# Splitting the merge's weights during the second token group instead of at their first use

## Chip, core and metric

The kernel runs on 1 core of one Trainium2 chip. The metric is device time in microseconds (us) of one execution. The time before is the median of three runs.

## What is computed

One layer of an encoder trunk on 2048 prompt tokens and 8 x 16 decode tokens (17 tiles of 128 tokens), all in float32. Every token gets one wide projection; three branches (a gated convolution, a gated linear recurrence, a causal stick-breaking attention) turn it into `o_a`, `o_b`, `o_c`; the merge at the end combines them. The change concerns the weights of the merge, `w_branch` (1536 x 1024) and `w_out` (1024 x 1024):

```python
    h = rms_norm(x, norm_g[l])
    (a_x, ..., s_z, m_a, m_b, m_c) = split_cols(h @ w_in[l])
    ...
    wb = w_branch[l]
    y_a = o_a @ wb[:W_CONV]
    y_b = o_b @ wb[W_CONV:W_CONV + W_HG]
    y_c = o_c @ wb[W_CONV + W_HG:]
    m = jax.nn.sigmoid(m_a) * y_a + jax.nn.sigmoid(m_b) * y_b + jax.nn.sigmoid(m_c) * y_c
    return x + m @ w_out[l], conv_new, S_new.astype(x.dtype), k, v
```

## The kernel before

**Products of float32 numbers.** Each float32 matrix is kept as two parts of type fp32r: `hi`, the value rounded by a cast on ScalarE (ACT), and `lo`, the rest, subtracted on VectorE (DVE). The helper `split` does both (lines 175 and 176). A product is then three passes on TensorE (PE): hi x hi, hi x lo, lo x hi.

**Weights.** `wload` fetches a weight piece of 512 KB. At its first use it comes as float32 into a staging buffer `wst` (two of them) and is split into a buffer `w` that holds both parts (1024 KB, three of them). `wkeep` then stores `w` to a tensor `W` in device memory, and later uses of the same piece load the two parts from there, without a split. Every fourth load of a kept piece goes into the two staging buffers instead of a `w` (the counter `turns`).

**Stages.** Three token groups (`GROUPS`: 5, 6 and 6 tiles) run the projection one after another, each in 64 jobs (72 weight pieces) on two chunks of tokens, so 128 turns to a group. The weights of the projection are split in the first group. The merge follows: four groups of tokens (`PGROUPS`: 5, 4, 4 and 4 tiles), each with 12 branch jobs (`bjob`, matmuls on line 1391, gating on DVE on lines 1397 to 1400) and 4 output jobs (`ojob`, matmuls on line 1422, one DVE addition on line 1430). Each merge group uses the same 20 weight pieces (12 of `w_branch`, 8 of `w_out`). Before the change the first merge group splits them, and the other three load parts.

**Work beside the jobs.** Generators run a slice of other work at each `yield` of a job: `hbg` the recurrence, `bg` the attention. During the second token group `bg` is the decode tokens' attention; from the third on it is the prompt's attention, in four query blocks, which the merge needs one by one. A step of it, for one tile of queries against up to 512 keys, is: two matmuls into `z` (lines 329, 330), two sigmoids on ACT (333, 335), a scan along the keys and a product on DVE (342, 347), four transposes on PE into `tp` (310), a copy on ACT (311), and later matmuls into `pv` (359). Each link waits for the one before.

**What sets the order.** The code only gives priorities. When the program is built, a scheduler lays out every engine's instructions in one fixed order, from the order of the code and its own reckoning of when data and buffers are ready. On the chip each engine, and the DMA queue of SyncE (SP), which issues all transfers, goes through its list strictly in that order and waits where something is missing. So a change to one stage's loads can also change which instructions stand next to each other.

Of the kernel before, what the change touches and what calls it, by code (L numbers as in the profile page):

```python
# [8 lines left out]
F32 = mybir.dt.float32  # L9
F32R = mybir.dt.float32r  # L10
# [6 lines left out]
P = 128  # L17
# [81 lines left out]
def trunk(ctx: ExitStack, tc: tile.TileContext, x_prompt, x_sample, cache_conv, state_hgrn, cache_k, cache_v,  # L99
# [3 lines left out]
    nc = tc.nc  # L103
# [25 lines left out]
    dram = ctx.enter_context(tc.tile_pool(name="dram", bufs=1, space=DRAM))  # L129
# [43 lines left out]
    def split(hi, lo, src, eng=None):  # L173

        first = nc.scalar.copy(hi, src)  # L175
        return first, (eng or nc.vector).tensor_tensor(lo, src, hi.bitcast(F32), ALU.subtract)  # L176
# [8 lines left out]
    kept = {}  # L185
    turns = [0]

    def wload(pieces, key):


        out = []
        for n, v in enumerate(pieces):
            a, b = v.shape[1], v.shape[2]
            if (key, n) in kept:
                turns[0] += 1
                if turns[0] % 4 == 0:

                    hl = []
                    for i in range(2):
                        x = wp.tile([P, a, b], F32, tag="wst", name="wst", bufs=2)  # L200
                        nc.sync.dma_start(x, kept[key, n][:, i].rearrange("p (a b) -> p a b", a=a).bitcast(F32))
                        hl.append(x.bitcast(F32R))
                    out.append((*hl, None))
                    continue
            w = wp.tile([P, 2, 1024], F32R, tag="w", name="w")
            hi, lo = (w[:, i].rearrange("p (a b) -> p a b", a=a) for i in range(2))
            if (key, n) in kept:
                nc.sync.dma_start(w.bitcast(F32), kept[key, n].bitcast(F32))
            else:
                st = wp.tile([P, a, b], F32, tag="wst", name="wst", bufs=2)  # L210
                nc.sync.dma_start(st, v)
                with ExitStack() as order:
                    if len(kept) < 1 and n:

                        for x in prep.last:
                            order.enter_context(tc.issue_after(x.ins))
                    split(hi, lo, st)
            out.append((hi, lo, w))
        return out
# [3 lines left out]
    def wkeep(out, key):  # L223
        for n, (_, _, w) in enumerate(out):
            if (key, n) not in kept:
                kept[key, n] = dram.tile([P, 2, 1024], F32R, name=f"W{len(kept)}")
                nc.sync.dma_start(kept[key, n].bitcast(F32), w.bitcast(F32))
# [519 lines left out]
    def build_vectors():  # L747
        nc.sync.dma_start(qg_bc, q_norm_g[0].partition_broadcast(P))
        nc.sync.dma_start(kg_bc, k_norm_g[0].partition_broadcast(P))

        vrow = g0p.tile([17, P], F32, tag="mtmp", name="vrow", bufs=2)
        nc.sync.dma_start(vrow[0:12], conv_w[0].rearrange("j (b p) -> (j b) p", p=P))
        nc.sync.dma_start(vrow[12:16], hg_lb_logits[0].rearrange("(h p) -> h p", p=P))
        nc.sync.dma_start(vrow[16:17], hg_norm_g)
        pvec = ps_tp()
        nc.tensor.transpose(pvec[:, 0:17], vrow, idf[0:17, 0:17])
        nc.vector.tensor_copy(vec, pvec[:, 0:17])
# [10 lines left out]
    def build_bound():  # L768
        lmax = const.tile([P, 4], F32, name="lmax")
        nc.vector.tensor_copy(lmax, vec[:, 12:16])  # L770
        lexp = const.tile([P, 4], F32, name="lexp")
        nc.vector.tensor_tensor(lexp, vec[:, 12:16], lmax, ALU.subtract)
        ebase = const.tile([P, 1], F32, name="ebase")
        nc.vector.memset(ebase, 2.718281828459045)
        nc.gpsimd.tensor_tensor(lexp, ebase.broadcast_to([P, 4]), lexp, ALU.pow)
        lsum = const.tile([P, 4], F32, name="lsum")
        nc.vector.reciprocal(lsum, lexp)
        lsm = const.tile([P, 4], F32, name="lsm")
        nc.vector.tensor_tensor(lsm, lexp, lsum, ALU.mult)
        nc.vector.tensor_tensor(lb, lsm, lsm, ALU.subtract)  # L780
        nc.vector.tensor_scalar(omlb, lb, -1.0, 1.0, ALU.mult, ALU.add)
# [22 lines left out]
    def build_rev():  # L804
        nc.gpsimd.memset(rev, 0.0)
        nc.gpsimd.affine_select(rev, rev, pattern=[[1, P]], base=1 - P, channel_multiplier=1,
                                compare_op=ALU.not_equal, fill=1.0)
# [39 lines left out]
    def build_hist():  # L847
        nc.gpsimd.memset(uhist, 0.0)
        nc.gpsimd.memset(shist, 0.0)
        nc.gpsimd.memset(cstage, 0.0)  # L850
        nc.sync.dma_start(cstage[0:16], cache_conv[0].rearrange("b t c -> (b t) c"))
# [407 lines left out]
    def run_late(cost):  # L1259
        for x in late:  # L1260
            x[0] -= cost
        for x in list(late):
            if x[0] <= 0:
                try:
                    x[0] = next(x[1])
                except StopIteration:
                    late.remove(x)

    def run_jobs(g, jobs):
        nonlocal prep  # L1270
        nxt = None
        n = len(jobs)
        ws = {}

        def weights(i):
            if i < n and i not in ws:
                ws[i] = wload(*jobs[i][0])

        order = [(i, ci) for i in range(2, n - 2) for ci in range(2)]
        begin = [(0, 0), (1, 0), (0, 1), (1, 1)] if g else [(0, 0), (0, 1), (1, 0), (1, 1)]  # L1280
        order = (begin + order
                 + [(n - 2, 0), (n - 1, 0), (n - 2, 1), (n - 1, 1)])
        for at_, (i, ci) in enumerate(order):
            weights(i)
            if g or at_:
                weights(i + 1)
            if not g and at_ == 0:
                prep.advance()
            if not g and at_ == 2:

                with tc.issue_after(rstd_at[0].ins), tc.issue_after(prep.last[1].ins):
                    build_vectors()
                    build_hist()
                    build_rev()
                    build_bound()
                    build_masks()
                    build_selectors()
            hT = prep.chunk(ci) if g or at_ > 1 else lambda ti, ci=ci: prep.tile(ci, ti)
            left = len(order) - at_
            if left == 5 and g + 1 < len(GROUPS):  # L1300
                nxt = Prepare(g + 1)
            for cost in jobs[i][1](ws[i], ci, hT):
                if at_ < 2:
                    prep.advance()
                    prep.advance()
                if nxt and (left <= 2 or nxt.ready < 0 and len(nxt.xt) < 3 or left <= 3 and not nxt.scaled):
                    nxt.advance()
                run_late(cost)
                hbg.run(cost * RATE_H)
                bg.run(cost * RATES[g] * jobs[i][2])  # L1310
            if ci == 0 and g < len(GROUPS) - 1:
                wkeep(ws[i], jobs[i][0][1])
        while late:
            run_late(1e9)
        hbg.drain()
        prep = nxt

    for g in range(len(GROUPS)):
        run_jobs(g, group_jobs(g))
        if g == 0:  # L1320
            p0.close()
            bg.add(sample_attention())
        if g == 1:
            prep.chunk(0)
            bg.drain()
            p01.close()
            open_attention()
            for qi in range(4):
                bg.add(attention(qi), key=qi)
# [4 lines left out]


    p3 = ctx.enter_context(tc.tile_pool(name="p3", bufs=1))
    wb = w_branch[0]
    wo = w_out[0]
    GMAX = max(sum(len(c) for c in pg) for pg in PGROUPS) * P

    def branch_w(x, dp):
        return ([wb[x * 512:(x + 1) * 512, dp * 256:(dp + 1) * 256].rearrange("(k p) m -> p k m", p=P)],
                ("branch", x, dp))

    def out_w(s):
        v = wo[:, s * 256:(s + 1) * 256].rearrange("(k p) m -> p k m", p=P)
        return [v[:, 0:4], v[:, 4:8]], ("out", s)

    def merge_jobs(gi):
        pg = PGROUPS[gi]  # L1350
# [85 lines left out]
    alljobs = []  # L1436
# [10 lines left out]
    ws = {0: wload(*alljobs[0][0])}  # L1447
    for i, (_, compute) in enumerate(alljobs):
        if i + 1 < len(alljobs):
            ws[i + 1] = wload(*alljobs[i + 1][0])  # L1450
        wkeep(ws[i], alljobs[i][0][1])
        for cost in compute(ws.pop(i)):
            bg.run(cost * RATE_M)
    bg.drain()
# [29 lines left out]
```

## Time and profile before

| what | value |
|---|---|
| median of 3 runs | 2918.34 us (2917.2 to 2919.45) |
| the profiled execution | 2918.2 us, of which the span from first to last instruction is 2916.1 us |
| mean granted TensorE clock | 0.997 |
| bytes moved by DMA | 624.58 MB, mean 214 GB/s |
| loads of kept weights | 153 of 1024 KB into `w`, 102 of 512 KB into `wst` (two for one piece) |
| stores of kept weights | 92 of 1024 KB |
| first merge matmul (line 1391) | 2188.8 us |
| last split of a weight starts | 2458.8 us |

The profile gives each engine's busy time. PE is matmuls, PEld their weight loads, which overlap with them; PEclk is the granted clock, 1.00 at full speed. "[1.36 <-DVE sp]" behind an instruction means that its engine stood idle 1.36 us before it, until DVE had written `sp`.

### The profile page before, as it was taken

The page shows a single profiled execution, that of the slowest core. Times are in us where ns is not written, and L with a number is a line of the kernel's source. Part 1 is how long each engine was busy: PE and PEld are TensorE (multiplying, and loading weights), DVE is VectorE, ACT ScalarE, POOL GpSimd, SP SyncE. Part 2 cuts the span into 40 slices and gives each one's busy share as a digit, 9 for nine tenths or more (in the row PEclk, how much of TensorE's full clock was granted, in tenths as well). Part 3 has the DMA queues.
Part 4 walks back from the last instruction along what each step waited for, and adds up shares of the span by engine and source line. Part 5 has one row for each costly group of instructions (what it writes and reads, how often), then busy time and mean ns, then how long its engine had stood idle before and what let it go on. Part 6 is the DMA issues. An engine that isn't in the chain of part 4 may idle for free.

```text
span 2916.1 us, 51581 instructions
## 1 busy us (share of the span) xinstructions
PE 2881.3 (99%) x19511; PEld 2673.5 (92%) x19511; DVE 1542.4 (53%) x3284; ACT 1020.2 (35%) x2371; POOL 322.5 (11%) x787
## 2 busy tenths in 40 slices
PE   9999999999999999999999999999998999999999
PEld 8999999999999999999999999999986777788888
DVE  5454644641352523345444748366575866867743
ACT  4333223242222222114333443334443444444420
POOL 3100000120100000002221111101011011110100
PEclk9999999999999999999999999999999999999999
DMA  8877777777556564536774454434438867888876
GB/s 307 306 259 247 234 229 242 246 237 246 187 185 213 175 220 149 166 138 192 248 219 159 153 160 156 149 128 166 131 118 276 271 227 257 297 264 262 274 258 218
DMA packets 355481, 624.58 MB, mean 214 GB/s; under 512 B 31929, under 2 KB 242706, under 8 KB 323874
## 3 DMA queue, kind: packets, MB, share of 16 engines
q1 hardware_dynamic: 355234, 621.29, 64.9%
q8 instruction: 155, 2.54, 0.3%
q14 instruction: 92, 0.75, 0.1%
HBM read 423.99 MB, written 197.17 MB: 213 GB/s over the span
## 4 chain that ended last, share of the span: by engine, by line
PE 75%; DVE 3%; DMA 1%; issue 1%; ACT 1%; POOL 0%; SPq 0%; DVEq 0%; POOLq 0%; ACTq 0%
PE acc L710 32%; PE acc L721 9%; PE acc L1391 9%; PE acc L1422 6%; PE pv L359 4%; PE tp L310 4%; PE z L329 2%; PE z L330 2%; PE z L1040 1%; DVE pr L342 1%; PE tp L458 1%; PE pv L522 1%; DMA xt<-in_x_prompt_dram 0%; PE z L476 0%; PE hg L1087 0%
## 5 line engine op out<-in xcount | busy, mean ns | idle before, releaser
L710 PE MATMUL acc<-hx,w 128*128 128x384 f32 (+1 forms) x6816 | 1254.7, 333 | 0.0
L710 PEld LDWEIGHTS acc<-hx,w 128*128 128x128 f32 x6816 | 1107.3, 188 | 22.2 <-issue 15.2
L721 PE MATMUL acc<-w,hx 128*128 128x256 f32 x2544 | 329.5, 284 | 1.7 <-DVE gm L1134 0.7
L342 DVE TENSOR_TENSOR_SCAN pr<-snb,carry 128x513 f32<-128x513 f32 x192 | 246.3, 1283 | 154.1 <-ACT snb L333 152.6
L721 PEld LDWEIGHTS acc<-w,hx 128*128 128x128 f32 x2544 | 311.4, 188 | 5.0 <-DVE hx L176 1.6
L311 ACT COPY aT<-tp 128x512 f32<-128x512 f32 (+2 forms) x320 | 167.0, 525 | 339.8 <-PE tp L310 331.6
L1391 PE MATMUL acc<-o,w 128*128 128x512 f32 (+2 forms) x1224 | 256.3, 360 | 5.6 <-DVE gate L1399 3.3
L710 PE MATMUL acc<-hx,wst 128*128 128x384 f32 x1248 | 247.3, 344 | 0.0
L1391 PEld LDWEIGHTS acc<-o,w 128*128 128x128 f32 x1224 | 207.0, 191 | 43.0 <-DVE gate L1399 9.0
L333 ACT ACTIVATE snb<-z 128x512 f32<-128x512 f32 (+2 forms) x320 | 172.5, 539 | 182.9 <-PE z L330 180.0
L710 PEld LDWEIGHTS acc<-hx,wst 128*128 128x128 f32 x1248 | 215.6, 188 | 6.4 <-issue 3.7
L347 DVE TENSOR_TENSOR sp<-sp,pr 128x512 f32<-128x512 f32 (+2 forms) x320 | 194.8, 610 | 25.4 <-PE tp L310 0.5
L342 DVE TENSOR_TENSOR_SCAN pr<-snb,one 128x129 f32<-128x129 f32 (+3 forms) x128 | 114.5, 895 | 133.9 <-POOL snb L338 133.2
L310 PE MATMUL tp<-idf,sp 128*128 128x128 f32 x1088 | 173.2, 275 | 6.3 <-DVE sp L347 5.1
L1422 PE MATMUL acc<-w,mh 128*128 128x256 f32 x896 | 175.4, 285 | 3.2 <-DVE w L176 2.4
L335 ACT ACTIVATE sp<-z 128x512 f32<-128x512 f32 (+2 forms) x320 | 171.8, 537 | 0.0
L176 DVE TENSOR_TENSOR w<-wst,w 128x1024 fp32r<-128x1024 f32 x92 | 112.5, 1224 | 111.7 <-ACT w L175 111.7
L310 PEld LDWEIGHTS tp<-idf,sp 128*128 128x128 f32 x1088 | 132.3, 142 | 30.5 <-ACT aT L311 8.6
L1422 PEld LDWEIGHTS acc<-w,mh 128*128 128x128 f32 x896 | 142.9, 188 | 11.6 <-issue 5.0
L1174 ACT ACTIVATE gm<-acc 128x384 f32<-128x384 f32 (+1 forms) x144 | 68.2, 474 | 232.9 <-PE acc L710 198.1
L359 PE MATMUL pv<-aT,Vt 128*64 128x512 f32 (+3 forms) x640 | 137.3, 541 | 1.6 <-ACT aT L311 1.6
L329 PE MATMUL z<-Kt,Q 128*128 128x512 f32 (+2 forms) x320 | 130.9, 410 | 2.7 <-ACT sp L335 2.6
(300 smaller groups left out, 3474.7 us busy)
## 6 DMA issues: line engine op xcount, KB each, us to landing
w<-W SPq DMA_DIRECT2D x153, 1024.0 KB, 5.3
W<-w SPq DMA_DIRECT2D x92, 1024.0 KB, 5.0
wst<-W SPq DMA_DIRECT2D x102, 512.0 KB, 5.0
wst<-in_w_in_dram SPq DMA_DIRECT2D x72, 512.0 KB, 6.3
GM<-gm SPq DMA_DIRECT2D x120, 192.0 KB, 3.4
Kt<-KT SPq DMA_DIRECT2D x160, 128.0 KB, 3.6
o<-OX SPq DMA_DIRECT2D x72, 256.0 KB, 4.7
gate<-GM SPq DMA_DIRECT2D x72, 256.0 KB, 4.1
```

The source lines that it names most:

```text
L310: nc.tensor.transpose(tp[:, j * P:(j + 1) * P], sp[:, j * P:(j + 1) * P], idf)
L311: nc.scalar.copy(aT[:, e, 0:nb, i * P:(i + 1) * P], tp[:, :w].rearrange("p (b q) -> p b q", q=P))
L329: nc.tensor.matmul(z[:, :w], Q1[:, i * P:(i + 1) * P], Kt[:, :w], start=True, stop=False)
L333: nc.scalar.activation(sn[:, 512 - w:512], z[:, :w], AF.Sigmoid, scale=-0.125)
L335: nc.scalar.activation(sp[:, :w], z[:, :w], AF.Sigmoid, scale=0.125)
L342: nc.vector.tensor_tensor_scan(pr[:, 512 - w:513][:, ::-1], s_in, s_in, one if diag else carry[e][i], ALU.mult, ALU.bypass)
L347: nc.vector.tensor_tensor(sp[:, :w], sp[:, :w], pr[:, 513 - w:513], ALU.mult)
L359: nc.tensor.matmul(pv[64 * e:64 * e + 64, c0:n], Vt[:, j, e], aT[:, e, j, c0:n], start=first and j == 0, stop=last and j == nb - 1, skip_g ...
L710: nc.tensor.matmul(acc[:, :n], w[0][a][:, k], hT[b][:, k, :n], start=k == 0 and i == 0, stop=k == KB - 1 and i == 2)
L721: nc.tensor.matmul(acc[:, :256], hT[b][:, k, ti * P:(ti + 1) * P], w[k // 4][a][:, k % 4], start=k == 0 and i == 0, stop=k == KB - 1 and i ...
L1391: nc.tensor.matmul(acc[:, :n], w[0][a][:, k, dd * P:(dd + 1) * P], box[x][b][:, k, sl], start=k == 0 and i == 0, stop=k == 3 and i == 2)
L1422: nc.tensor.matmul(acc[:, :256], box["l" if b else "h"][:, k, ti * P:(ti + 1) * P], w[k // 4][a][:, k % 4], start=k == 0 and i == 0, stop= ...
```

## The change

The 20 pieces of the merge are loaded as float32, split and stored while the second token group runs. A new generator `split_merge_weights` works on half a piece at a time (512 numbers to a partition), in three turns: load, split, store. It has its own two buffers, one float32 half `mwx` and one pair of parts `mwp`. There are 40 halves, so 120 turns, and `run_jobs` calls it once in each of the turns 4 to 123 of the second group. The pool `mw` is opened after the first group and closed after the second. In the merge every load of a weight, in the first group too, is then one of kept parts, and the loop no longer calls `wkeep`. Lines below the insertion move by 28 to 29: the merge's matmuls stand on lines 1420 and 1451, the new loads on 1292, the new stores on 1297.

```diff
+    def split_merge_weights():
+
+        mw = mwx.enter_context(tc.tile_pool(name="mw", bufs=1, side="right"))
+        yield
+        for pieces, key in [branch_w(x, dp) for x in range(3) for dp in range(4)] + [out_w(s) for s in range(4)]:
+            for n, v in enumerate(pieces):
+                kept[key, n] = dram.tile([P, 2, 1024], F32R, name=f"W{len(kept)}")
+                a, b = v.shape[1], v.shape[2]
+                for half in range(2):
+                    x = mw.tile([P, 512], F32, tag="mwx", name="mwx")
+                    nc.sync.dma_start(x.rearrange("p (a b) -> p a b", b=b), v[:, half * a // 2:(half + 1) * a // 2])
+                    yield
+                    w = mw.tile([P, 2, 512], F32R, tag="mwp", name="mwp")
+                    split(w[:, 0], w[:, 1], x)
+                    yield
+                    nc.sync.dma_start(kept[key, n][:, :, half * 512:(half + 1) * 512].bitcast(F32), w.bitcast(F32))
+                    yield
...
+            if g == 1 and 4 <= at_ < len(order) - 4:
+                next(splitting, None)
...
         if g == 0:
             p0.close()
+            next(splitting)
             bg.add(sample_attention())
         if g == 1:
             prep.chunk(0)
             bg.drain()
+            for _ in splitting:
+                pass
+            mwx.close()
             p01.close()
...
             ws[i + 1] = wload(*alljobs[i + 1][0])
-        wkeep(ws[i], alljobs[i][0][1])
         for cost in compute(ws.pop(i)):
```

(`branch_w` and `out_w` are moved up unchanged.)

**Where instructions stand now.** PE's list is the same up to a few places at the start of the second group, then the same until the merge begins, and differs over the first merge group; the later merge groups stand as before. The first place is on PE in the first merge group, behind about 150 branch matmuls. `z` and `tp` belong to attention steps, `pv` to their last product, `acc` to the merge. Before:

```order
L1391 MATMUL acc<-o,w 128x384 x12
L330 MATMUL z<-Kt,Q_24210 128x512
L329 MATMUL z<-Kt,Q_24209 128x512
L330 MATMUL z<-Kt,Q_24210 128x512
L310 MATMUL tp<-idf,sp 128x128 x4
L359 MATMUL pv<-aT,Vt 64x512
L329 MATMUL z<-Kt,Q_24209 128x512
L330 MATMUL z<-Kt,Q_24210 128x512
L310 MATMUL tp<-idf,sp 128x128 x12
L359 MATMUL pv<-aT,Vt 64x512 x4
L1391 MATMUL acc<-o,w 128x256 x12
```

and now, as many branch matmuls into the merge:

```order
L1420 MATMUL acc<-o,wst 128x256 x6
L310 MATMUL tp<-idf,sp 128x128 x4
L1420 MATMUL acc<-o,w 128x384 x6
L329 MATMUL z<-Kt,Q_25628 128x384
L330 MATMUL z<-Kt,Q_25629 128x384
L1420 MATMUL acc<-o,w 128x384 x6
L310 MATMUL tp<-idf,sp 128x128 x4
L1420 MATMUL acc<-o,w 128x256 x6
L329 MATMUL z<-Kt,Q_25628 128x512
L330 MATMUL z<-Kt,Q_25629 128x512
L1420 MATMUL acc<-o,w 128x256 x6
```

Before, four sets of transposes and the products stood together with no merge matmul between them; now six merge matmuls stand between the links of a step.

The second place is SP's list where the merge begins (`wst<-in_w_branch_dram` are the float32 weights, `W<-w` their store, `o` the branch outputs, `gate` the gates). Before:

```order
L211 DMA wst<-in_w_branch_dram 128x4x256
L1175 DMA GM<-gm 128x384
L211 DMA wst<-in_w_branch_dram 128x4x256
L287 DMA Kt<-KT 64x512
L1361 DMA o<-OX 128x640 x8
L227 DMA W_25099<-w 128x2048
L1383 DMA gate<-GM 128x640 x2
```

and now:

```order
L208 DMA w<-W_7901 128x2048
L1175 DMA GM<-gm 128x384 x2
L287 DMA Kt<-KT 64x512 x2
L1175 DMA GM<-gm 128x384
L1098 DMA out_dram<-Sn 128x128
L291 DMA Vt<-VV 128x4x128
L208 DMA w<-W_8363 128x2048
L1175 DMA GM<-gm 128x384
L182 DMA OX<-oh 128x256
L182 DMA OX<-ob 128x256
L201 DMA wst<-W_8911 128x1024
```

The weights of the first four branch jobs are now issued ahead of the merge, among the last stores of the third token group, and no store of weights follows.

The third place is ACT's list in the second token group (`vf` are evacuations of a projection job, `at` and `od` belong to the decode attention). One piece of the difference:

```order
 L836 COPY vf<-acc 128x256 x2
 L175 CAST kt<-hg 128x256
-L501 COPY at__8105<-tp 128x384
-L836 COPY vf<-acc 128x256 x4
+L501 COPY at__8128<-tp 128x384
+L836 COPY vf<-acc 128x256 x3
+L175 CAST mwp<-mwx 128x512
+L836 COPY vf<-acc 128x256
 L527 COPY od<-pv 128x128
```

A cast of half a weight piece now stands between two evacuations of the accumulators.

More of the change, by code (lines that the diff above doesn't have):

```diff
@@ L1267, in run_late, with branch_w, out_w @@
                     late.remove(x)
+    wb = w_branch[0]
+    wo = w_out[0]
+    mwx = ExitStack()
+    def branch_w(x, dp):
+        return ([wb[x * 512:(x + 1) * 512, dp * 256:(dp + 1) * 256].rearrange("(k p) m -> p k m", p=P)],
+                ("branch", x, dp))
+    def out_w(s):
+        v = wo[:, s * 256:(s + 1) * 256].rearrange("(k p) m -> p k m", p=P)
+        return [v[:, 0:4], v[:, 4:8]], ("out", s)
+    def split_merge_weights():
[14 more added lines that the diff above has]
+                    yield
+    splitting = split_merge_weights()
     def run_jobs(g, jobs):
@@ L1336, in trunk @@
     p3 = ctx.enter_context(tc.tile_pool(name="p3", bufs=1))
-    wb = w_branch[0]
-    wo = w_out[0]
     GMAX = max(sum(len(c) for c in pg) for pg in PGROUPS) * P
[L1341 to L1347, printed above, removed]
     def merge_jobs(gi):
```

## Prediction

> **What bounds the kernel now.** I read the page's first part, then a table of the stages, then, where PE stands idle, the waits and the timeline. The page:
>
> ```profile
> span 2916.1 us, 51581 instructions
> PE 2881.3 (99%) x19511; PEld 2673.5 (92%) x19511; DVE 1542.4 (53%) x3284; ACT 1020.2 (35%) x2371; POOL 322.5 (11%) x787
> ```
>
> PE is busy 2881.3 of 2916.1 us, and the change takes no matmul away, so all there is to win is PE's idle time (34.8 us) and what a lowered clock costs. Where these lie, by stage (stretch in us, its length, then busy time of PE, PEld, DVE, ACT, POOL with counts, the granted clock, DMA share, GB/s):
>
> ```profile
> 620.00:1330.00 710.00, 710.00 (x5298) 690.46 (x5297) 256.60 (x746) 182.37 (x489) 43.10 (x84) 1.00 0.57 186
> 2180.00:2190.00 10.00, 7.81 (x41) 5.03 (x41) 9.23 (x10) 9.08 (x17) 0.55 (x3) 0.99 0.88 279
> 2190.00:2360.00 170.00, 155.00 (x880) 123.06 (x879) 115.32 (x186) 69.65 (x141) 20.88 (x51) 0.96 0.80 263
> 2360.00:2470.00 110.00, 107.93 (x731) 91.91 (x732) 72.44 (x92) 49.22 (x92) 9.88 (x31) 1.00 0.76 254
> 2470.00:2847.00 377.00, 377.00 (x2220) 306.45 (x2219) 256.47 (x342) 151.19 (x302) 34.25 (x111) 1.00 0.81 269
> ```
>
> The first row is the second token group, where the splits go: PE never idle. Rows two to four are the first merge group and its outputs, where the splits come from: idle 2.19, 15.00 and 2.07 us, over half of all idle time, in a tenth of the span. The last row is the rest of the merge with the same attention beside it and no splits: idle 0. Who is waited for, between 2180 and 2470 us (total, times, longest):
>
> ```profile
> PE tp L310 <- DVE sp L347: 5.1, 7, 1.4
> PE acc L1391 <- DVE gate L1399: 3.3, 2, 2.4
> PE z L329 <- ACT sp L335: 2.6, 3, 2.1
> PE acc L1422 <- DVE w L176: 2.4, 2, 1.3
> PE acc L1391 <- DVE mp L1397: 2.2, 2, 1.9
> PE pv L359 <- ACT aT L311: 1.6, 3, 0.7
> ```
>
> Only the fourth row names a split. The others are the links of an attention step and the gating behind them on DVE. The timeline shows the first kind (start, duration, engine, line):
>
> ```profile
> 2223.12 0.69 DVE L347 TENSOR_TENSOR sp<-sp,pr 128x512 f32<-128x512 f32 x1
> 2223.73 1.28 DVE L342 TENSOR_TENSOR_SCAN pr<-snb,carry 128x513 f32<-128x513 f32 x1
> 2223.96 1.08 PE L310 MATMUL tp<-idf,sp 128*128 128x128 f32 x4 [1.36 <-DVE sp L347]
> 2225.12 0.69 DVE L347 TENSOR_TENSOR sp<-sp,pr 128x512 f32<-128x512 f32 x1
> 2225.96 1.09 PE L310 MATMUL tp<-idf,sp 128*128 128x128 f32 x4 [0.91 <-DVE sp L347]
> 2227.72 3.42 PE L359 MATMUL pv<-aT,Vt 128*64 128x512 f32 x8 [0.68 <-ACT aT L311]
> ```
>
> DVE needs 1.28 + 0.69, about 2 us, for a step; PE's transposes of it are done in half of that, and then PE has nothing: its list holds twelve transposes and the products in a row (the order of before above). So PE goes at DVE's pace, and the clock falls too:
>
> ```profile
> 2190.00:2200.00 10.00, 10.00 (x47) 7.19 (x48) 6.24 (x7) 2.97 (x6) 0.00 (x0) 0.84 1.02 356
> 2220.00:2230.00 10.00, 6.72 (x22) 3.00 (x24) 6.29 (x8) 4.39 (x9) 0.00 (x0) 0.70 1.07 277
> 2230.00:2240.00 10.00, 9.77 (x52) 6.25 (x49) 2.42 (x5) 2.87 (x8) 2.27 (x7) 0.96 0.16 64
> 2340.00:2350.00 10.00, 7.58 (x35) 5.58 (x34) 6.23 (x14) 3.61 (x9) 2.47 (x6) 0.84 0.37 116
> ```
>
> The clock is below full by 1.6, 3.0, 0.4 and 1.6 us in these four slices, 6.6 in all. Idle time at a low clock must not be counted twice: 3.28 x 0.30 + 2.42 x 0.16 = 1.4 off, so 5.2 us. What can be regained in 2190 to 2470 is thus 15.0 + 2.1 + 5.2 = 22.3 us.
>
> [...]
>
> **The change part by part.**
>
> *1. The first merge group loses its splits.* Rows of the splits, whole and as an existing 512-wide split has them (busy, mean ns | idle before), and DVE's and ACT's work on `wst` in the stretch:
>
> ```profile
> L175 ACT CAST w<-wst 128x1024 fp32r<-128x1024 f32 x92 | 96.8, 1052 | 66.5 <-PE acc L710 24.4 <-DMA wst<-in_w_in_dram 12.8 <-DMA wst<-in_w_branch_dram 11.7
> L176 DVE TENSOR_TENSOR w<-wst,w 128x1024 fp32r<-128x1024 f32 x92 | 112.5, 1224 | 111.7 <-ACT w L175 111.7
> L175 ACT CAST oth<-ot 128x512 fp32r<-128x512 f32 x16 | 9.9, 620 | 54.0 <-DVE ot L366 54.0
> L176 DVE TENSOR_TENSOR ot<-ot,oth 128x512 fp32r<-128x512 f32 x16 | 11.0, 689 | 7.5 <-ACT oth L175 7.5
> ...
> 2190.00:2360.00 170.00, 0.00 (x0) 0.00 (x0) 13.28 (x11) 12.74 (x12) 0.96 0.80 263
> ```
>
> 20 pieces x 1.224 = 24.5 us leave DVE and 20 x 1.052 = 21.0 us leave ACT, beside PE, so nothing of it counts by itself. ACT also no longer stands in line for the float32 pieces: 11.7 us of idling in its list, with attention steps behind.
>
> *2. PE's list is laid out anew in this group.* This is the part that counts. Of the two lists above, the new one keeps six merge matmuls between the links of a step. I went through all of both lists: from the merge's start on, the old one has eleven places with three or more attention steps, or twelve or more transposes, in a row without a merge matmul; the new one has one, at the very start, where PE waits for `o` in both. Bounds for what comes back: 0 (the waits only move) and all 22.3 us. The nearest row for the new state is 2470 to 2847: the same interleaving, no idle time, clock 1.00, with DVE at 256.47 / 377 = 68%. The first group would have DVE at (115.32 - 13.28) / (170 - 20) = 68%, so it should come near that row. A second reading: PEld is busy 123.06 / 170 = 72% here and 306.45 / 377 = 81% there; at 81% the 170 us would shrink by 18.6.
>
> [...]
>
> I take 80% of 22.3, 17.8 us, and leave 4.5 for what I expect to stay: the 1.6 of clock after the wait for `o`, and places where gates come late, since ninety merge matmuls now stand in a row where `o` has landed:
>
> ```profile
> 2200.69 1.35 DVE L1397 TENSOR_TENSOR mp<-acc,gate 128x384 f32<-128x384 f32 x3 [4.06 <-DMA gate<-GM]
> ...
> w<-W SPq DMA_DIRECT2D x153, 1024.0 KB, 5.3
> W<-w SPq DMA_DIRECT2D x92, 1024.0 KB, 5.0
> gate<-GM SPq DMA_DIRECT2D x24, 320.0 KB, 4.8
> wst<-in_w_branch_dram SPq DMA_DIRECT2D x12, 512.0 KB, 5.8
> kc<-in_cache_k_dram SPq DMA_DIRECT2D x64, 256.0 KB, 4.1
> ```
>
> *3. Transfers of the first merge group.* 20 x 512 KB in and 20 x 1024 KB out become 20 x 1024 KB in: 30 MB become 20, and SP has 20 issues fewer that waited for DVE. A load of parts lands after 5.3 us, a float32 piece after 5.8 and then two splits' time. The first four jobs' loads stand ahead of the merge. Price 0; if a job's weights came late each time, 5.3 us x a few jobs, which is in the high end.
>
> *4. The wait at 2180 to 2190 us.* The first merge matmul needs `o`, loaded once the last gates are stored, in both orders. PE gets two more attention steps into the wait. Bounds: 0 to 2.2 us regained, a loss of as much if a step ends after `o` has come. I take 0.
>
> *5. The second token group gains the splits.* 40 casts x 0.620 = 24.8 us on ACT, 40 x 0.689 = 27.6 us on DVE, 80 transfers (40 x 256 KB in, as the row of 4.1 us, 40 x 512 KB out). ACT goes from 182 to 207 and DVE from 257 to 284 us of 710, 29% and 40%. The cover is PE's own work: ACT's evacuations wait for PE there, not PE for them. SP's weight loads likewise wait for PE to free a buffer, so they are early. In that group:
>
> ```profile
> ACT gm L1174 <- PE acc L710: 102.0, 41, 4.5
> SPq L208 <- PE acc L710: 95.3, 23, 10.7
> ```
>
> ACT is early by 102.0 / 41 = 2.5 us on the mean. A cast of 0.62 us and a wait for its load (in the first group 12.8 us for 72 casts, 0.18 each) fit in. The new store waits on SP for DVE's half, one turn after it was given out; behind it stand weight loads with 4.1 us to spare (95.3 / 23). With no cover at all the price is 40 x (0.62 + 0.18) = 32 us; nothing excludes a microsecond of gain or loss from the few matmuls moved at this group's start. I take +0.5.
>
> *Sum.* -17.8 + 0 + 0.5 = -17.3 us on the profiled execution of 2918.2 us (span 2916.1, 2.1 around it), which stands 0.1 under the median of 2918.34: 2901 us.
>
> **The rivals.**
>
> *A, as summed:* 2901, own range 2893 to 2908.
>
> *B, the denser list meets transfers:* with PE quicker, gates (two buffers, 4.8 us each) or parts become what PE waits for. For it: DMA share 0.80 and the 4.06 us wait. Against it: 2470 to 2847 has a share of 0.81 and no idle time. Half of the 17.8 is lost: 2909.
>
> *C, the waits move:* five of six rows of waits name attention and gating, not splits; if DVE's chain stays in PE's way, only row four (2.4 us) and its clock go: 2915. For it: the rows. Against it: the chain of 2 us a step is the same from 2470 on, where it costs nothing.
>
> *D, slower: ACT blocks in the second group.* A cast waits for `mwx`, whose load can stand on SP behind a weight load that waits for PE, up to 10.7 us; evacuations stand behind the cast on ACT, and PE stops when its two accumulators are full. It decides from 17.8 / 40 = 0.45 us of PE per half; at 1 us each the time is 2901 + 40 = 2941. For it: the single `mwx` and the cast between evacuations. Against it: ACT's 2.5 us, and the first group's 0.18.
>
> **How the numbers follow.** A 0.65, B 0.15, C 0.12, D 0.08. The likeliest is A, 2901. Faster than 0.2% (5.8 us, about what a measurement of this kernel can tell, so below 2912.5): A, and nearly all of B, 0.78. Within 0.2%: nearly all of C and the rest of B, 0.14. Slower: D, 0.08. The range reaches from everything regained with the wait of part 4 and its clock (2918.2 - 22.3 - 2.2 - 2, about 2891) up to B with some loss in the second group (2913); that leaves out C and D, 0.2.
>
> **What would show it.** In the changed kernel's profile: PE's idle time and clock in the first merge group near those of 2470 to 2847; no row of PE waiting for a split after the first token group; PE busy 710 of 710 in the second group, with ACT and DVE 25 and 28 us up; the same times for the stages after the first merge group. B would show as PE or DVE waiting for `gate` or `w` at the merge, C as the same waits for `sp` and `aT`, D as idle time of PE in the second group with ACT's casts waiting for `mwx`.

## The result and the profile after

| | before | after |
|---|---|---|
| median of 4 runs of each on one chip | 2917.77 us | 2902.40 us (2896.27 to 2903.30) |
| ratio | | 0.9943, 95% interval 0.9926 to 0.9961 |
| profiled execution, its span | 2918.2, 2916.1 us | 2896.3, 2894.6 us |

15.4 us faster by the medians, 21.5 by the two spans: the profiled execution of after is the quickest of its four, 6 us under the other three. The total is near the 2901 forecast by luck: the merge gained about twice as much as the sum said, and the second token group gave nearly half of it back. The first lines of the page after:

```profile
span 2894.6 us, 51726 instructions
PE 2864.3 (99%) x19511; PEld 2671.5 (92%) x19511; DVE 1547.5 (53%) x3304; ACT 1025.5 (35%) x2391; POOL 317.0 (11%) x787
```

PE has the same 19511 matmuls and is busy 17 us less. So "busy" held time that was no work, and the page alone can't say where it went. Landmarks do: when a line's instructions start for the last or the first time. Rows of lines and tiles (count, min/median/max ns, first to last start); before, the last transpose of a token group's input (the third's, which is done while the second group ends), the last projection matmul, the first branch matmul, the first output matmul:

```profile
L629 PE MATMUL tp<-idf,xt x136: 270/272/329, 8.0 to 1349.6; 128*128 128x128 f32 x136
L710 PE MATMUL acc<-hx,wst x1248: 331/337/449, 663.4 to 2180.0; 128*128 128x384 f32 x179
L1391 PE MATMUL acc<-o,w x1224: 274/390/667, 2188.8 to 2861.3; 128*128 128x512 f32 x92, 128*128 128x384 f32 x43, 128*128 128x256 f32 x40
L1422 PE MATMUL acc<-w,mh x896: 274/281/390, 2358.1 to 2911.2; 128*128 128x256 f32 x180
```

and after:

```profile
L629 PE MATMUL tp<-idf,xt x136: 270/273/421, 8.0 to 1366.5; 128*128 128x128 f32 x136
L710 PE MATMUL acc<-hx,wst x1248: 331/337/444, 668.0 to 2196.2; 128*128 128x384 f32 x179
L1420 PE MATMUL acc<-o,w x1080: 274/392/482, 2206.2 to 2839.7; 128*128 128x512 f32 x108, 128*128 128x384 f32 x38, 128*128 128x256 f32 x34
L1451 PE MATMUL acc<-w,mh x816: 274/281/387, 2343.1 to 2889.6; 128*128 128x256 f32 x164
```

| stretch | before | after | change |
|---|---|---|---|
| start to the end of the second group (last x-transpose) | 1349.6 | 1366.5 | +16.9 |
| from there to the last projection matmul | 830.4 | 829.7 | -0.7 |
| to the first branch matmul | 8.8 | 10.0 | +1.2 |
| to the first output matmul | 169.3 | 136.9 | -32.4 |
| to the end | 558.0 | 551.5 | -6.5 |

**Where the second group lost 17 us.** Its row in the table of stages, which was 710 of 710 busy, and PE's waits between 560 and 1380 us:

```profile
620.00:1330.00 710.00, 698.20 (x5197) 676.11 (x5196) 270.45 (x754) 198.51 (x517) 43.54 (x84) 1.00 0.68 226
```

```profile
PE hg L827 <- DVE kt L176: 7.1, 4, 3.0
PE tp L1089 <- ACT ktm L1053: 2.5, 3, 1.2
PE tp L629 <- DVE xt L619: 2.5, 3, 1.3
PE tp L629 <- DVE hx L176: 2.1, 1, 2.1
PE acc L721 <- ACT kn L815: 1.3, 1, 1.3
```

PE now waits for small jobs of ACT and DVE that used to be early: 18.1 us with the smaller rows, against 5.6 before. The clock adds 3.4 us at most, an estimate from 2 x 3.41 us at one half (at 591 and 793 us); before, it is at full speed throughout this group. The waits of ACT and DVE name what holds those two:

```profile
ACT mwp L175 <- DMA mwx<-in_w_branch_dram: 56.6, 23, 5.6
ACT mwp L175 <- DMA mwx<-in_w_out_dram: 44.4, 16, 4.7
DVE mwp L176 <- ACT mwp L175: 108.0, 36, 25.0
```

39 of the 40 casts stand at the head of ACT's list before their data has landed: 101.0 us in 39 waits, 2.6 us each. DVE stands behind the same casts; no run separates its list from ACT's. The timeline of one case (start, duration, engine, line):

```profile
634.88 0.62 ACT L175 CAST mwp<-mwx 128x512 fp32r<-128x512 f32 x1 [3.61 <-DMA mwx<-in_w_branch_dram]
635.40 0.38 ACT L813 ACTIVATE sq<-acc 128x256 f32<-128x256 f32 x1
635.93 0.39 ACT L175 CAST kt<-hg 128x256 fp32r<-128x256 f32 x1
637.38 0.41 DVE L817 TENSOR_REDUCE ssq<-sq 128x4 f32<-128x256 f32 x1
637.49 0.53 SPq L1297 DMA_DIRECT2D W<-mwp  x1
638.11 0.56 SPq L1292 DMA_DIRECT2D mwx<-in_w_branch_dram  x1
639.20 0.42 DVE L820 TENSOR_TENSOR kn<-kn,rr 128x256 f32<-128x256 f32 x1 [1.41 <-POOL rr L234]
...
640.00 0.41 DVE L176 TENSOR_TENSOR kt<-hg,kt 128x256 fp32r<-128x256 f32 x1
640.47 0.44 PE L827 MATMUL hg<-idf,kn 128*128 128x128 f32 x2 [2.99 <-DVE kt L176]
642.60 0.62 ACT L175 CAST mwp<-mwx 128x512 fp32r<-128x512 f32 x1 [4.07 <-DMA mwx<-in_w_branch_dram]
```

ACT waits 3.61 us for a half's load, and only behind its cast come the squares `sq` and the cast of `kt`. DVE's sum `ssq`, GpSimd's `rr`, DVE's `kn` and the rest of `kt` follow one by one, and PE stands idle for 2.99 us until `kt` is done. That this wait of PE goes back to ACT's is read from the order of the lists. Meanwhile SP issues the next load right behind the last half's store, and ACT waits 4.07 us for it; behind that wait PE has no idle time until 648 us, so not every wait of ACT costs PE. Nor are the splits spread as the code's turns are:

```profile
L175 ACT CAST mwp<-mwx x40: 617/620/626, 584.0 to 1089.6; 128x512 fp32r<-128x512 f32 x40
```

The last of the 40 runs at 1089.6 us, though its turn in the code is near the group's end at about 1300. That fits a scheduler that takes a split forward as soon as it reckons that the load is there; on the chip it isn't.

**Where the merge gained.** The same 600 branch matmuls, from the first of them to the first output matmul, before and after (columns as in the table of stages):

```profile
2188.80:2358.10 169.30, 155.47 (x884) 123.72 (x883) 114.72 (x186) 68.95 (x141) 19.61 (x49) 0.96 0.80 263
2206.20:2343.10 136.90, 135.31 (x862) 117.32 (x863) 101.77 (x169) 55.12 (x118) 12.70 (x44) 1.00 0.83 274
```

Of the 32.4 us, idle time gives 12.2 (13.8 to 1.6). The other 20.2 were booked as busy: about 22 attention matmuls that now run elsewhere (884 to 862 in all), the lowered clock, and longer records of the same matmuls (the 78 into `pv` are busy 24.7 us in this stretch before, 17.6 in e3_gain's). How the 20.2 divides among these was not measured, and the clock has a part in the longer records too.

### The profile page after: what moved, and what is told of

Its sections match the earlier page's. It is cut to its first block, busy times and chain, and to the rows that moved or that the text cites. A ratio compares the mean times of both kernels' runs of the same rounds, so it can differ in the third digit from the quotient of the medians.

```text
span 2894.6 us, 51726 instructions
## 1 busy us (share of the span) xinstructions
PE 2864.3 (99%) x19511; PEld 2671.5 (92%) x19511; DVE 1547.5 (53%) x3304; ACT 1025.5 (35%) x2391; POOL 317.0 (11%) x787
## 4 chain that ended last, share of the span: by engine, by line
PE 73%; DMA 3%; DVE 3%; issue 1%; ACT 1%; POOL 1%; SPq 0%; ACTq 0%; DVEq 0%; POOLq 0%
PE acc L710 31%; PE acc L1420 10%; PE acc L721 8%; PE acc L1451 7%; PE pv L359 4%; PE tp L310 4%; PE z L330 2%; PE z L329 2%; DMA mwx<-in_w_branch_dram 1%; PE z L1040 1%; PE tp L458 1%; DMA mwx<-in_w_out_dram 1%; PE pv L522 1%; DMA GM<-gm 0%; PE z L476 0%
## 5 line engine op out<-in xcount | busy, mean ns | idle before, releaser
L1420 PE MATMUL acc<-o,w 128*128 128x512 f32 (+2 forms) x1080 | 234.6, 363 | 1.1 <-DMA o<-OX 1.1
L1420 PEld LDWEIGHTS acc<-o,w 128*128 128x128 f32 x1080 | 184.9, 188 | 33.0 <-issue 4.5
L1451 PE MATMUL acc<-w,mh 128*128 128x256 f32 x816 | 160.5, 284 | 0.0
L176 DVE TENSOR_TENSOR w<-wst,w 128x1024 fp32r<-128x1024 f32 x72 | 88.1, 1224 | 106.3 <-ACT w L175 106.2
L1451 PEld LDWEIGHTS acc<-w,mh 128*128 128x128 f32 x816 | 130.7, 188 | 5.8 <-issue 4.2
L359 PE MATMUL pv<-aT,Vt 128*64 128x512 f32 (+3 forms) x640 | 128.1, 535 | 0.0
```

The lines of the kernel that those rows point to most:

```text
L359: nc.tensor.matmul(pv[64 * e:64 * e + 64, c0:n], Vt[:, j, e], aT[:, e, j, c0:n], start=first and j == 0, stop=last and j == nb - 1, skip_g ...
L1420: nc.tensor.matmul(acc[:, :n], w[0][a][:, k, dd * P:(dd + 1) * P], box[x][b][:, k, sl], start=k == 0 and i == 0, stop=k == 3 and i == 2)
L1451: nc.tensor.matmul(acc[:, :256], box["l" if b else "h"][:, k, ti * P:(ti + 1) * P], w[k // 4][a][:, k % 4], start=k == 0 and i == 0, stop= ...
```

## The experiments

Each kernel was timed beside the kernel before on the same chip; "ratio" is to that, with its 95% interval. Before's medians in the three sets were 2917.7, 2917.9 and 2918.2 us. Where an expectation counts bunched places in PE's list, it counts one at the end of the second token group as well.

### The gain alone and the cost alone

**e3_gain**: in the generator, only this is left of the loop's inside:

```diff
-                kept[key, n] = dram.tile([P, 2, 1024], F32R, name=f"W{len(kept)}")
-                ... (load, split, store of two halves)
+                kept[key, n] = old[len(kept) - len(old)]     # a kept piece of the projection
```

> The gain alone: nothing of the merge's weights is loaded, split or stored in the second group; the merge loads kept parts of the projection's weights in their place, as many bytes at the same places (so it computes with other weights). Theory of two terms that cancel (merge gains about 38 us by the traces, second group loses 16): 2880 to 2886. The sum as predicted (merge -17.8, second group +0.5): about 2900.

Measured: 2879.32 us, ratio 0.9866 (0.9851 to 0.9881). -38.4 us, not -17.8.

**e4_cost**: the halves are stored to spare tensors, and the merge works as before:

```diff
-                kept[key, n] = dram.tile([P, 2, 1024], F32R, name=f"W{len(kept)}")
+                spare = dram.tile([P, 2, 1024], F32R, name=...)
...
+        wkeep(ws[i], alljobs[i][0][1])
         for cost in compute(ws.pop(i)):
```

> The cost alone: the second group loads, splits and stores the halves as in the changed kernel, but into tensors that nobody reads; the merge loads float32 pieces, splits and stores them as before. Two cancelling terms: 2918 + 16 = about 2934. The sum as predicted (+0.5 for the second group): about 2918.

Measured: 2935.68 us, ratio 1.0058 (1.0045 to 1.0071). +18.0 us, not +0.5. The second group's rows, gain alone and cost alone:

```profile
620.00:1330.00 710.00, 710.00 (x5297) 690.43 (x5296) 256.46 (x746) 183.28 (x491) 42.20 (x83) 1.00 0.56 186
```

```profile
620.00:1330.00 710.00, 697.23 (x5185) 674.41 (x5183) 269.04 (x752) 197.18 (x515) 43.45 (x84) 1.00 0.68 226
```

So the two terms are there separately. Together they make -20.4, where the whole change measured -15.4 by the medians and -21.5 by the spans; those 5 us stay open.

### What the second group pays for

**e1_pin** keeps all work, transfers and buffers, and holds each split in its turn:

```diff
                     yield
+                    yield
                     w = mw.tile([P, 2, 512], F32R, tag="mwp", name="mwp")
-                    split(w[:, 0], w[:, 1], x)
+                    act = next(i for i in reversed(nc.cur_bb.bb.instructions) if i.engine == mybir.EngineType.Activation)
+                    with tc.issue_after(act):
+                        split(w[:, 0], w[:, 1], x)
                     yield
                     nc.sync.dma_start(kept[key, n][:, :, half * 512:(half + 1) * 512].bitcast(F32), w.bitcast(F32))
-                    yield
```

(`issue_after` sets the order of issue on one engine, without a wait.)

> The changed kernel, but each split is given out two turns after its load and held behind the ACT instruction given out last, so that its data should have landed before ACT comes to the cast; work, transfers and buffers are the same. Theory 1 (the second group loses about 16 us because ACT's casts stand in its list ahead of their data, 2.6 us each, and evacuations stand behind them): the second group is back to about 745 us between the first decode scores and the last x-transpose, total about 2888. Theory 2 (the loss is the added work and traffic itself: 40 casts, 40 subtractions, 80 transfers): no change, about 2902.

Measured: 2882.06 us, ratio 0.9874 (0.9861 to 0.9888). 20 us faster than the changed kernel, 35.7 faster than before, within 3 us of the gain alone, and 6 under theory 1's 2888. Its second group, its casts, and the one wait for `mwx` that is left:

```profile
620.00:1330.00 710.00, 710.00 (x5296) 690.41 (x5295) 279.98 (x786) 202.22 (x529) 42.72 (x83) 1.00 0.70 230
L175 ACT CAST mwp<-mwx x40: 610/622/642, 635.3 to 1308.4; 128x512 fp32r<-128x512 f32 x40
ACT mwp L175 <- DMA mwx<-in_w_out_dram: 1.5, 1, 1.5
```

ACT and DVE are busier than in the changed kernel's stretch (202 and 280 against 199 and 270 us, since more of the splits fall into it), the DMA share is higher (0.70 against 0.68), and PE has no idle time. The work and the traffic are hidden, as forecast; what cost was the place of the splits in the engines' lists.

**e11_pin1** has the hold without the second turn.

```diff
-                    split(w[:, 0], w[:, 1], x)
+                    act = next(i for i in reversed(nc.cur_bb.bb.instructions) if i.engine == mybir.EngineType.Activation)
+                    with tc.issue_after(act):
+                        split(w[:, 0], w[:, 1], x)
```

> The changed kernel with load, split and store in the turns where it has them, and each split held behind the ACT instruction given out last, so that it can't be moved forward past its own turn: one turn (about 5.5 us) behind its load in place of two. If what counts is that a cast isn't taken forward to the point where its data is only reckoned to be there: most of the loss goes, 2882 to 2890, with a few waits for mwx left. If one turn is too short on this chip: 2892 to 2900.

Measured: 2883.48 us, ratio 0.9882 (0.9869 to 0.9894); two waits for `mwx` are left, 2.8 us together. The hold does it; the code's one turn was lead enough once the casts stayed in their turns.

Three attempts to take the wait away without holding the casts missed.

**e2_apart**:

```diff
-                    split(w[:, 0], w[:, 1], x)
+                    split(w[:, 0], w[:, 1], g_bc[:, :512])
```

> The changed kernel with the same loads, casts, subtractions and stores, but the casts read a constant tile instead of the loaded half, so that no cast waits for a load (the merge then computes with other weights). Theory 1: the 16 us go, about 2887. Theory 2 (work and traffic): about 2902, as before this edit.

Measured: 2897.05 us, ratio 0.9923 (0.991 to 0.9935). 2887 was expected and only a quarter of the 20 us came: the casts moved forward until the next thing that was reckoned ready too early, the buffer behind the last store.

```profile
L175 ACT CAST mwp<-g_bc x40: 615/620/632, 542.7 to 994.1; 128x512 fp32r<-128x512 f32 x40
ACT mwp L175 <- DMA W<-mwp: 94.2, 36, 5.5
```

**e6_free** takes that link away too:

```diff
-                    nc.sync.dma_start(kept[key, n][...].bitcast(F32), w.bitcast(F32))
+                    nc.sync.dma_start(kept[key, n][...].bitcast(F32), g_bc.rearrange("p (a b) -> p a b", b=512))
```

> As the kernel whose casts read a constant, and the stores read a constant as well, so that neither the loaded half nor the pair of parts is waited for by anyone; casts, subtractions, loads and stores are all there (the merge computes with other weights). Theory 1, mended: there the wait only moved, from the load of mwx to the store of mwp (94.2 us in 36 waits); with both gone the second group costs nothing and the time is about 2880 to 2882. Theory 2 (work and traffic cost the rest): about 2897, as with the one link gone.

Measured: 2896.55 us, ratio 0.9928 (0.9914 to 0.9941), a miss for 2880 to 2882. It doesn't speak for theory 2, since now nothing held the splits at all: the casts of two 40 us windows around the group's start (length, busy, count, clock, DMA share, GB/s):

```profile
560.00:600.00 40.00, 11.84 (x19) 0.96 0.80 266
600.00:640.00 40.00, 9.94 (x16) 1.00 0.65 220
```

35 of 40 casts run there, among the evacuations where the two groups meet. Work that waited for nothing wasn't spread here; it was taken forward. So this kernel measures splits in one heap, and not splits without waits. The heap, in which no cast waits for a transfer, costs 17 us against the gain alone; so whether the waits themselves cost the changed kernel its 18 us, or splits that run ahead of their turns, is not separated. e1_pin took both away.

**e5_inplace**: two `mwx`, each loaded one half ahead, the rest written into the loaded half:

```diff
+            x = mw.tile([P, 512], F32, tag="mwx", name="mwx", bufs=2)
...
-                    w = mw.tile([P, 2, 512], F32R, tag="mwp", name="mwp")
-                    split(w[:, 0], w[:, 1], x)
+            w = mw.tile([P, 512], F32R, tag="mwp", name="mwp")
+            split(w, x.bitcast(F32R), x)
```

> The changed kernel with two buffers for the loaded half (each loaded one half ahead; the rest is written into the loaded half itself, so the room is the same), and no split held in its place. If loading earlier were enough: 2880 to 2886. By what the two kernels with constants showed, the scheduler takes the casts forward until the next thing that it reckons ready too early, here the buffer behind the last store: 2893 to 2902.

Measured: 2907.51 us, ratio 0.9964 (0.9952 to 0.9976), outside both, and 5 us slower than the changed kernel. Its waits, 102.7 us again, now of three kinds:

```profile
ACT mwp L175 <- DMA W<-mwp: 60.7, 21, 6.1
ACT mwp L175 <- DMA mwx<-in_w_branch_dram: 25.6, 10, 4.2
ACT mwp L175 <- DMA mwx<-in_w_out_dram: 16.4, 7, 4.1
```

The earlier load was no help here: its lead went into earlier casts.

### What the merge gained from

The prediction gave the gain to the splits' leaving PE's list. Four kernels take the first merge group apart: work of the splits, stores, traffic of the stores.

**e7_work** adds to e3_gain the work alone:

```diff
+        if i < 16:
+            for half in range(2 * len(ws[i])):
+                scr = p3.tile([P, 512], F32R, tag="scr", name="scr", bufs=1)
+                split(scr, scr, g_bc[:, :512])
         for cost in compute(ws.pop(i)):
```

> The gain alone (no splits in the second group, parts loaded in the merge), and in the first merge group 40 splits of 512 numbers from a constant into a scratch tile that nobody reads: ACT and DVE do the work that the first merge group did before, and nobody waits for it. Theory S (the stores of the parts were what spoilt PE's list): PE's list keeps its interleaving, the time stays at 2879 to 2882. Theory W (the splits' 25 us of ACT and 28 us of DVE stood in the attention's chain): a good part of the 38 us is lost again, 2890 to 2905.

Measured: 2885.05 us, ratio 0.989 (0.9876 to 0.9903): 5.7 us of the 38, outside both ranges: 3 us above that of S, 5 below that of W.

**e8_stores** adds to e3_gain the stores alone:

```diff
+            for n, (hi, lo, w) in enumerate(ws[i]):
+                dst = dram.tile([P, 2, 1024], F32R, name=f"S{i}_{n}")
+                if w is not None:
+                    nc.sync.dma_start(dst.bitcast(F32), w.bitcast(F32))
+                ... (else: the two staging buffers, one by one)
```

> The gain alone, and in the first merge group each piece of loaded parts is stored once more (20 x 1024 KB, to tensors that nobody reads), where the kernel before stored its split pieces; no split there. Theory S: a store holds its weight buffer in the scheduler's reckoning, the next weights come later in it, and PE's list has fourteen places with attention steps in a row and no merge matmul (two without the stores): 2905 to 2918. Theory W (the splits' work was the cost): 2879 to 2883, with the stores hidden.

Measured: 2926.42 us, ratio 1.0034 (1.0021 to 1.0047): 47 us slower than e3_gain, 8 over the range, and slower than the kernel before. Who is waited for on PE, 2180 to 2470 us, here:

```profile
PE tp L310 <- DVE sp L347: 8.9, 8, 2.3
PE pv L359 <- ACT aT L311: 3.8, 6, 0.7
PE acc L1410 <- DVE gate L1418: 3.0, 5, 1.4
```

They are the attention links and the gating that the kernel before showed, though no weight is split in this group. No row of PE's waits names a weight.

**e12_traffic** stores the same 20 MB from a constant tile, so that no store holds a weight buffer:

```diff
-                if w is not None:
-                    nc.sync.dma_start(dst.bitcast(F32), w.bitcast(F32))
-                ...
+                for v in range(2):
+                    nc.sync.dma_start(dst[:, v].bitcast(F32), g_bc)
```

> The gain alone, with the same 20 MB stored in the first merge group as in the kernel with stores, but from a constant tile, as two stores of 512 KB for a piece, so that no store holds a weight buffer; PE's list keeps its interleaving (two bunched places). Theory S1 (the stores cost by the buffers that they hold, and so by PE's list): 2879 to 2886. Theory S2 (the stores cost by their traffic, beside loads, gates and attention's keys): 2905 to 2925.

Measured: 2879.44 us, ratio 0.9869 (0.9856 to 0.9881). The traffic costs 0.1 us. In e8_stores a store also reads weights that a load has to bring first, and what stands behind it on SP may come later by that (not measured); e12_traffic takes that away as well, so the two are not told apart.

**e10_nostore** takes the stores out of the kernel before, and leaves the splits where they were:

```diff
-        wkeep(ws[i], alljobs[i][0][1])
+        for n in range(len(ws[i])):
+            if (alljobs[i][0][1], n) not in kept:
+                kept[alljobs[i][0][1], n] = old[len(kept) - len(old)]
```

> The kernel before without the stores of the merge's parts: the first merge group still loads float32 pieces and splits them, and the later groups load kept parts of the projection's weights (so they compute with other weights). Theory S: PE's list has three bunched places in place of twelve, and most of the merge's gain comes without any move of the splits: 2880 to 2890. Theory W: about 2915, as before.

Measured: 2885.35 us, ratio 0.9891 (0.9877 to 0.9904): 32.6 of the 38.4 us without moving a split. The stretch from 2190 to 2360 us, stores alone and splits without stores:

```profile
2190.00:2360.00 170.00, 153.65 (x889) 125.12 (x887) 103.99 (x177) 57.28 (x128) 18.54 (x56) 0.97 0.86 284
```

```profile
2190.00:2360.00 170.00, 168.84 (x1088) 146.52 (x1087) 139.15 (x214) 84.36 (x165) 22.85 (x62) 1.00 0.76 239
```

DVE is busiest where PE is fullest (139 us against 104), so DVE's load was not the limit. What goes with the time is the list: with stores of weight buffers 11 (before) or 13 (e8_stores) bunched places in the merge, without them 1 or 2 (e3_gain, e7_work, e12_traffic; e10_nostore). The bytes cost 0.1 us (e12_traffic), and the work about 5.7 (e7_work). The list was not changed alone. Why e8_stores is 8.5 us slower than the kernel before, with no weight split in the group, stays open beyond its two bunches more. That the scheduler makes the bunches because it reckons the next weights late while a store holds their buffer fits all of this, but was not measured by itself.

## Why the prediction was right in its total and wrong in its terms

The total is luck: part 2 was off by -20.6 us and part 5 by +17.5, and these two nearly cancel.

- **Part 2, the re-laid list (-17.8): mis-sized, and its cause misnamed.** The mechanism, bunches giving way to an interleaved list, is what happened. The size is -38.4 (e3_gain). The step that failed is the pool of 22.3 us: it held PE's idle time and the lowered clock, and a busy row can't show the rest. Before to after, the stretch of the 600 branch matmuls lost 12.2 us of idle time and 20.2 of "busy" time. The second reading, PEld's share, failed by its target: the stage taken as the model has 81%, the first merge group came to 117.32 / 136.90 = 86%. At 86% the formula gives 170 - 123.06 / 0.857 = 26 us, nearer, still short. Over the 600 branch matmuls PEld's share moved from 73% to 86%, and PE's from 92% to 99%.
- **Whose the bunches were.** The prediction spoke of the splits. It had the issues "that waited for DVE" in part 3 and priced them at 0; the runs put 32.6 of the 38.4 us on the stores (e10_nostore).
- **Part 1, splits hidden (0):** nearly right, about 5.7 us (e7_work).
- **Part 3, transfers (0):** right for the traffic (0.1 us, e12_traffic), wrong for stores out of weight buffers.
- **Part 4, the wait for `o` (0):** 8.8 us became 10.0, within the bounds.
- **Part 5, the second group (+0.5): wrong.** It costs 18.0 (e4_cost). The failed step is "a wait for its load (0.18 each) fits in": the 0.18 came from the first group, and here it was 2.6 us in 39 of 40 casts. ACT's mean lead of 2.5 us is shorter than that wait and the cast together. The other half of the step held: without the waits the same work and traffic are hidden (e1_pin).
- **Rival D** named the place, casts that wait for `mwx`, and the cost, 18.0 / 40 = 0.45 us of PE per half, is just the point from which it was said to decide. It didn't decide only because the other term was twice its forecast. At 0.08 it was held too unlikely. Its way there is not what the trace shows. The load did not stand on SP behind a blocked one: in 35 of the 39 waits its issue began before ACT's wait, in the other four at most 0.73 us after, and the cast came 3.1 to 7.8 us behind the issue. Nor did PE stop at full accumulators: the one row above that names a projection's evacuation (`kn`) is 1.3 us of 18.1. **B** and **C** did not occur: PE's waits from 2180 to 2470 us, after, are these two and two under half a microsecond:

```profile
PE tp L310 <- ACT aT L311: 1.6, 1, 1.6
PE acc L1420 <- DMA o<-OX: 1.1, 1, 1.1
```

- **What would show it** gave the verdict on part 5 at once: PE is not 710 of 710 in the second group, and D's sign, waits for `mwx`, is there.

## What to carry to other kernels

Where a scheduler fixes the order at build time, a new piece of work can cost by its place in an engine's list more than by its duration: here a cast put ahead of its data stopped the engine for 2.6 us where its own work is 0.62, and holding it in its turn gave 19 to 20 us back. Price a wait from the queue and the lead of its own stage, not from a stage that looks alike; and a store that only writes something away was followed by another order on an engine that never touches the store, probably by the buffer that it holds. When a total comes out right, compare landmarks stage by stage: here -38 and +18 stood behind a forecast of -17.3.

## What the hardware showed unexpectedly

Four 2 us windows in a row of the kernel before, in the bunched place that the prediction's timeline shows:

```profile
2222.00:2224.00 2.00, 0.64 (x5) 0.43 (x6) 1.90 (x3) 1.24 (x3) 0.00 (x0) 0.98 1.05 214
2224.00:2226.00 2.00, 1.09 (x5) 0.72 (x6) 1.90 (x3) 0.58 (x1) 0.00 (x0) 0.50 1.13 209
2226.00:2228.00 2.00, 1.32 (x6) 0.93 (x8) 0.61 (x2) 0.58 (x1) 0.00 (x0) 0.50 0.96 291
2228.00:2230.00 2.00, 2.00 (x6) 0.48 (x6) 0.00 (x0) 0.00 (x0) 0.00 (x0) 0.50 1.09 442
```

The clock is at one half, 0.50, from 2223.9 us on; PE's longest single wait in these windows is 1.36 us, with matmuls between the waits. Within the spans of before and after the clock records hold only 1.00 and 0.50, and half speed lasts 3.41 us, or once two times that: in the merge of the kernel before from 2189.8 us, from 2223.9 (6.83 us) and from 2346.8. The values of 0.70 and 0.84 in the prediction's rows were means over 10 us of full and half. The longest matmul into `pv` in that stage took 1112 ns, against 644 in e3_gain. The 3.41 us ahead of each of the three places:

```profile
2186.39:2189.80 3.41, 1.38 (x8) 1.18 (x9) 3.41 (x4) 2.98 (x6) 0.00 (x0) 1.00 0.99 329
2220.51:2223.93 3.42, 1.75 (x8) 0.72 (x6) 3.21 (x5) 2.71 (x6) 0.00 (x0) 1.00 1.06 207
2343.40:2346.81 3.41, 1.51 (x8) 1.04 (x7) 2.28 (x4) 2.59 (x7) 1.95 (x4) 1.00 0.11 41
```

PE was busy for 40 to 51% of them. What lowers the clock was not tried by a run.
